# Products over six weight rows in the second MLP matrices, with weight sums made by adding transfers

## The chip, the cores and the metric

The kernel runs on one core of a Trainium2 chip. A core has a matrix engine (TensorE, PE in the profile), a vector engine (VectorE, DVE), an activation engine (ScalarE, ACT), a general engine (GpSimd, POOL) and a queue engine (SyncE, SP); each runs its own list of instructions in order and waits for the others by semaphores. Sixteen DMA engines move data between the chip's memory (HBM) and the core's memory (SBUF); sums of matmuls are held in PSUM, in banks of 128 x 512 float32. The metric is the device time of one execution in microseconds (us), less is better.

## The reference

A two-layer encoder over 256 tokens of width 2048, 16 heads of 128, an MLP of width 8192 in each layer, all in float32:

```python
u = rms_norm(h, a_norm_g[l]); proj = u @ a_w_in[l]           # q, k, v and forget gates
o = forgetting_attention(rms_norm(q), rms_norm(k), v, logf)  # causal, decay bias
h = h + o @ a_w_out[l]
h = h + sq_relu_mlp(h, mlp_norm_g[0], mlp_w1[0], mlp_w2[0])  # (relu(x @ w1) ** 2) @ w2
k_sh, v_sh = split(rms_norm(h, kv_norm_g) @ kv_w)
q = rms_norm(rms_norm(h, b_norm_g[l]) @ b_w_q[l])
o = chunked_relbias_attention(q, k_sh, v_sh, b_rel[l])       # relative position bias
h = h + o @ b_w_out[l]
h = h + sq_relu_mlp(h, mlp_norm_g[1], mlp_w1[1], mlp_w2[1])
```

## The kernel before

**Three passes for float32.** Each matrix operand is cut into a high part and the rest. For a weight tile `issue` (L175) lets ScalarE copy it with rounding into `hi` (L184) and VectorE subtract that into `lo` (L185). A product is then the three passes of `passes` (L402): high by high (L408), high by low activation (L410), low weight by high activation (L412).

**Units.** A weight unit is a tile of 128 x 1024: two weight rows (input tiles of 128) of one output panel of 512 columns. With two blocks of 128 tokens and three passes, `products` (L416) makes twelve matmuls of 512 columns from it. `fetch` (L188) keeps splits up to three units ahead (`AHEAD`), and loads of raw tiles by SP three further. The pool `wsp` has three buffers of `hi` and `lo`, so a split waits until TensorE is through with the unit three before.

**Pairs and formed products.** In the MLP two output panels form a `Pair` (L119). For the first four input tiles (the 2 x 2 blocks of two weight rows by two panels, and two pairs of activation tiles by two token blocks) the pair computes seven products in place of eight, after Strassen and Winograd: "11", T3, T2, T1, "21", T4, "22" (`Form`, L107). T1 to T4 are sums of the weight blocks that VectorE makes (`make`, L747); the sums of the activations come from `sums` (L230). `form_products` (L435) makes six matmuls of one. The remaining input tiles go through plain units, six for each panel (a2 to a7 and b2 to b7).

**The order** is written out: `plan_mlp` (L132) sets the formed products f0 to f6 between the plain units; the last three units of the pair ahead (b5 to b7) lie between f0, f1, f2 and f3. `prepare` (L762) brings the four weight blocks of the next pair (`bring`, L742) and makes T1 and T3 when a given number of plain units is left (`Pair.units`). Two copies of a bank by ScalarE (L853, L856) and two additions by VectorE (L837, L845) join the products in PSUM; the copies stand behind the unit that follows their product. At the end of a matrix panel, VectorE takes the banks (L278, L528), and a list of small tasks, `fill`, is worked off one entry per plain unit (`run_fill`, L197): turning the hidden values by way of DRAM, squaring, splitting, sums.

**Chunks.** The hidden width of 8192 goes in four chunks of 2048; a chunk has two pairs of the first matrix and two of the second, so that a layer's MLP has 16 pairs and the kernel 32.

**The attention** runs as `fill` tasks under the projections. Its biases are loaded by SP (`decay_bias` L709 from a row `cd` written at L695, `rel_bias` L886), into a tile `bias` with two buffers. `begin` (L621) loads and splits the input at the start. POOL has some powers for the head norms (L492) and a few memsets.

Of the kernel before, what the change touches and what calls it, by code (L numbers as in the profile page):

```python
# [31 lines left out]
REL = 384  # L32

# [13 lines left out]
def trunk(ctx: ExitStack, tc: tile.TileContext, xT, xr, gs, hg, bf, wgate, w_in, w_oa, w1a, w2a,  # L47
          w_kv, w_qb, w_ob, w1b, w2b, rel, out):
# [23 lines left out]
    def load_x(i):  # L72
        raw_x[i] = qkv.tile([P, GH, T], F32, name="xin", tag="kv"[i // 2], bufs=2)
        SY.dma_start(raw_x[i], xT[:, i * GH : (i + 1) * GH, :])
# [3 lines left out]
    load_x(0)  # L78

# [4 lines left out]
    ones = const.tile([P, T], F32, name="ones")  # L84
    V.memset(ones, 1.0)
    warm = ps_o.tile([P, 512], F32, name="pt", tag="po")
    for _ in range(11):
        TE.matmul(warm[:, :P], ones[:, :P], ones[:, :P], start=True, stop=True)
# [30 lines left out]
    class Pair:  # L119
# [3 lines left out]
        def __init__(self, src, first, order, third):  # L123
            self.src = [[src[first + q * 8 + u] for u in range(8)] for q in range(2)]
            self.third, self.ps, self.t, self.room, self.units = third, None, {}, None, (9, 8, 7, 6, 5, 2)
            self.head = {"early": "a2 f4 a3 f5 b2 f6 b3 a4 b4 a5 a6 a7", "late": "a2 f4 a3 f5 b2 f6 b3 a4 a5 b4 a6 a7",
                         "": "a2 f4 a3 f5 a4 f6 a5 a6 a7 b2 b3 b4"}[order]

        def items(self, names):
            return [(self, "abf".index(i[0]), int(i[1])) for i in names.split()]  # L130

    def plan_mlp(w1, w2, tail):  # L132
        n, pairs = w1.shape[0] // NCH, []
        for c in range(NCH):
            for src, late in ((w1, ""), (w2, "late")):
                for q in range(2):
                    pairs.append(Pair(src, c * n + 16 * q, (late if pairs else "early") if q == 0 else "", len(pairs) % 2 == 0))
        pairs[0].units, pairs[1].units, pairs[2].units = (15, 13, 11, 8, 10, 8), (9, 8, 7, 6, 3, 2), (9, 8, 7, 6, 1, 2)
        plan, rest = [], [(tail, 0, u) for u in range(KT // UA - 3, KT // UA)]
        for p in pairs:  # L140
            f = p.items("f0 f1 f2 f3")
            plan += [f[0], rest[0], f[1], rest[1], f[2], rest[2], f[3]] + p.items(p.head)
            rest = p.items("b5 b6 b7")
        plan += rest
        units.extend(Form(p, i) if q == 2 else p.src[q][i] for p, q, i in plan)
        return plan
# [6 lines left out]
    plan_a = plan_mlp(w1a, w2a, tail_a)  # L153
# [5 lines left out]
    plan_b = plan_mlp(w1b, w2b, tail_b)  # L159
# [15 lines left out]
    def issue(parts=1):  # L175
        if not raws:
            load(parts)
        raw, cuts = raws.popleft()
        if not cuts:
            raw, cuts = raw.pair.t[raw.name], [slice(0, UN)]  # L180
        hi = wsp.tile([P, UN], F32R, name="hi")
        lo = wsp.tile([P, UN], F32R, name="lo")
        for c in cuts:
            S.activation(hi[:, c], raw[:, c], AF.Copy)  # L184
            V.tensor_tensor(lo[:, c], raw[:, c], hi[:, c].bitcast(F32), op=ALU.subtract)  # L185
        ready.append((hi, lo))

    def fetch(ahead=AHEAD, early=EARLY):  # L188
        while (units or raws) and len(ready) <= ahead:
            issue()  # L190
        while units and sum(1 for r in raws if r[1]) < early:
            load()
        return ready.popleft()
# [36 lines left out]
    def sums(a, fs):  # L230

        w = [wk.tile([P, 512], F32, name="sum", tag="wk") for _ in range(2)]

        def part(i):
            v = w[i // 2][:, i % 2 * 256 : i % 2 * 256 + 256].rearrange("p (g t) -> p g t", g=2)
            return v.rearrange("p g (i c) -> p g i c", i=4) if len(a[0][0].shape) == 4 else v

        V.tensor_tensor(part(0), a[1][0], a[1][1], op=ALU.add)
        V.tensor_tensor(part(1), part(0), a[0][0], op=ALU.subtract)
        V.tensor_tensor(part(2), a[0][0], a[1][0], op=ALU.subtract)  # L240
        V.tensor_tensor(part(3), a[0][1], part(1), op=ALU.subtract)
        hi, lo = ([fs[k][:, i * 512 : (i + 1) * 512] for i in range(2)] for k in range(2))
        for i in range(2):
            S.activation(hi[i], w[i], AF.Copy)
        yield
        for i in range(2):
            V.tensor_tensor(lo[i], w[i], hi[i].bitcast(F32), op=ALU.subtract)
        yield

    def split_turned(t, n, which, into, fs=None):  # L250
        x = acts.tile([P, 2, GH, T], F32R, name="act")
        y = qkv.tile([P, GH, REL], F32, name="bias")[:, :, :T]
# [45 lines left out]
    def turned(name="q"):  # L298
        z = qkv.tile([P, GH * T], F32, name="z")
        return z, qkv.tile([P, GH * T], F32, name=name, tag=name, bufs=2)  # L300
# [52 lines left out]
    class RowStats:  # L353
# [27 lines left out]
        def spread(self):  # L381
            self.R = const.tile([P, T], F32, name="R")
            pr = ps_o.tile([P, 512], F32, name="pt", tag="po")
            rb = wk.tile([P, NB, P], F32, name="rb", tag="wk")
            for b in range(NB):
                V.tensor_scalar(rb[:, b], ones[:, :P], self.r[:, b : b + 1], None, op0=ALU.mult)
# [48 lines left out]
    def form_products(ps, hi, lo, x, fs, i):  # L435
        items = []
        for g in range(2):
            if i in (0, 4, 5):
                xp = [x[2 * g + (i > 0)][:, k, (i == 5) * P : (i == 5) * P + P] for k in range(2)]
            else:  # L440
                c = {3: 0, 2: 1, 1: 2, 6: 3}[i] * 256 + g * P
                xp = [fs[k][:, c : c + P] for k in range(2)]
            items.append((ps[i not in (4, 5)][i in (1, 5)], xp, g, i < 2 and g == 0, i < 2 and g == 1))
# [177 lines left out]
    def begin(u):  # L621
        if u == 0:
            load(2)
            load(2)
# [24 lines left out]
    wgr = const.tile([P, KT * H], F32, name="wgr")  # L649
    ct = {}  # L650

    def gates(x, st):
# [5 lines left out]
        def clear():  # L658
            G.memset(w.bitcast(F32), 0.0)

# [11 lines left out]
        c = const.tile([H, T], F32, name="gc")  # L672

        def logs():
# [14 lines left out]
            V.tensor_tensor_scan(c, ones[:H, :], z, 0.0, op0=ALU.mult, op1=ALU.add)  # L689
# [5 lines left out]
            SY.dma_start(ct["cd"], nct)  # L695
            yield

        def turn_c():
            pc = ps_o.tile([P, 512], F32, name="pt", tag="po")
            ct["cq"] = const.tile([P, NB, H], F32, name="cq")  # L700
            for b in range(NB):
# [5 lines left out]
                [step], [step], [step], [step], [], [turn_c]]  # L707

    def decay_bias(g, box):  # L709
        nb = qkv.tile([P, GH, REL], F32, name="bias")  # L710
        src = ct["cd"][g * GH : (g + 1) * GH, :]
        SY.dma_start(nb, src.unsqueeze(0).to_broadcast([P, GH, REL]))
# [10 lines left out]
    for g in range(NG):  # L723
# [12 lines left out]
        zk, k = turned("k")  # L736
        v = qkv.tile([P, NB, 512], F32, name="v")
# [4 lines left out]
    def bring(p, name):  # L742
        t = qkv.tile([P, UN], F32, name="w" + name, tag="kv"[name[1] == "2"], bufs=2)
        SY.dma_start(t, p.src[int(name[1]) - 1][int(name[0]) - 1])
        p.t[name] = t

    def make(p, name):  # L747
        t = p.t
        if name in ("T1", "T3"):
            if p.room is not None:  # L750
                t[name] = p.room[:, (name == "T3") * UN : (name == "T3") * UN + UN]
            else:
                t[name] = qkv.tile([P, GH * REL], F32, name="w" + name, tag="bias", bufs=2)[:, :UN]
        elif name == "T2":
            t[name] = t["12"]
        else:
            t[name] = t["11"]
        a, b, op = {"T1": ("12", "11", ALU.subtract), "T3": ("22", "12", ALU.subtract),
                    "T2": ("T3", "11", ALU.add), "T4": ("21", "T2", ALU.subtract)}[name]
        V.tensor_tensor(t[name], t[a], t[b], op=op)  # L760

    def prepare(p, d):  # L762
        if d == p.units[0] and p.units[0] > 9:
            p.room = prob.tile([P, 9 * 3 * P], F32, name="wTT", tag="p", bufs=1)
        for name, at in zip(("12", "11", "22", "21", "T1", "T3"), p.units):
# [209 lines left out]
```

## Time and profile before

| | |
|---|---|
| median of 3 runs | 2109.41 us (2108.85 to 2110.25) |
| the profiled execution, its time | 2109.01 us |
| the profiled execution, its span | 2107.2 us |
| TensorE busy in the span | 2099.1 us |
| HBM read, written | 450.01 MB, 39.87 MB |
| mean rate of the DMA engines | 233 GB/s |
| granted clock of TensorE | 1.000 |

The page gives busy times of each engine, then groups of instructions as "line engine operation, out<-in, shapes, count | busy us, mean ns of one | idle before, and what ended it". PE rows overlap by the depth of their pipeline, so that the step from the start of one row to the start of the next is the time to count with. The rows themselves stand in the prediction, where they are used.

### The profile page before, as it was taken

To read this page: it belongs to the slowest core of one execution; us is meant where nothing else is said; L and a number is where in the kernel's file an instruction comes from. 1 tells how busy PE (TensorE), PEld (TensorE's weight loads), DVE (VectorE), ACT (ScalarE), POOL (GpSimd) and SP (SyncE) were. 2 spreads that over 40 slices of the span, in tenths; PEclk is the share of its full clock that TensorE was granted. 3 is DMA by queue.
4 is the path that set the end of the run, shared out by engine and by line. 5 is a ranking of instruction groups with operands and counts; after the bars stand their busy time and mean duration, and the time that the engine had idled before them with its cause. 6 is when DMAs were issued, how large, how long until landed. Compare 5 with 4: busy or idle time off the path is not lost.

```text
span 2107.2 us, 26036 instructions
## 1 busy us (share of the span) xinstructions
PE 2099.1 (100%) x9332; PEld 1741.2 (83%) x9332; DVE 1587.3 (75%) x1812; ACT 1191.4 (57%) x1431; POOL 48.7 (2%) x47
## 2 busy tenths in 40 slices
PE   9999999999999999999999999999999999999999
PEld 8788888888888888888888888888888888888887
DVE  6777676887788777778767677678877877887775
ACT  6545455665466565556575455456654654665653
POOL 1001000000000000000001000000000000000000
PEclk9999999999999999999999999999999999999999
DMA  8787778776676676577678777787766666766774
GB/s 289 236 257 231 234 250 272 241 238 231 216 241 212 211 250 230 188 245 259 194 242 259 238 233 233 227 279 240 257 227 202 232 230 217 236 216 210 244 239 146
DMA packets 182594, 491.63 MB, mean 233 GB/s; under 512 B 36784, under 2 KB 74048, under 8 KB 182464
## 3 DMA queue, kind: packets, MB, share of 16 engines
q1 hardware_dynamic: 182464, 489.96, 71.2%
q8 instruction: 73, 1.20, 0.2%
q14 instruction: 57, 0.47, 0.1%
HBM read 450.01 MB, written 39.87 MB: 232 GB/s over the span
## 4 chain that ended last, share of the span: by engine, by line
PE 99%; DMA 1%; SPq 0%; ACT 0%; DVE 0%; issue 0%; DVEq 0%; ACTq 0%
PE acc L408 26%; PE acc L410 26%; PE acc L412 26%; PE s L408 6%; PE s L412 6%; PE s L410 6%; DMA raw<-in_w_in 1%; PE po L581 1%; PE s L550 1%; PE po L582 0%; PE s L549 0%; PE s L670 0%; DMA turn<-z 0%; SPq L294 0%; ACT hi L184 0%
## 5 line engine op out<-in xcount | busy, mean ns | idle before, releaser
L185 DVE TENSOR_TENSOR lo<-raw,hi 128x1024 fp32r<-128x1024 f32 (+1 forms) x642 | 778.3, 1216 | 296.8 <-ACT hi L184 286.5
L184 ACT ACTIVATE hi<-raw 128x1024 fp32r<-128x1024 f32 (+1 forms) x642 | 677.6, 1057 | 515.2 <-PE acc L410 394.7
L408 PE MATMUL acc<-hi,act 128*128 128x512 f32 x2306 | 632.9, 393 | 2.9 <-ACT hi L184 2.9
L410 PE MATMUL acc<-hi,act 128*128 128x512 f32 x2306 | 623.8, 389 | 0.0
L412 PE MATMUL acc<-lo,act 128*128 128x512 f32 x2306 | 623.5, 389 | 0.0
L410 PEld LDWEIGHTS acc<-hi,act 128*128 128x128 f32 x2306 | 432.8, 188 | 90.4
L412 PEld LDWEIGHTS acc<-lo,act 128*128 128x128 f32 x2306 | 432.8, 188 | 89.9
L408 PEld LDWEIGHTS acc<-hi,act 128*128 128x128 f32 x2306 | 430.8, 188 | 90.9 <-ACT hi L184 3.8
L184 ACT ACTIVATE hi<-w 128x1024 fp32r<-128x1024 f32 x160 | 169.5, 1059 | 153.8 <-PE acc L410 94.4
L185 DVE TENSOR_TENSOR lo<-w,hi 128x1024 fp32r<-128x1024 f32 x160 | 194.8, 1218 | 69.3 <-ACT hi L184 68.3
L408 PE MATMUL s<-hi,act 128*128 128x512 f32 x448 | 121.1, 389 | 0.0
L410 PE MATMUL s<-hi,act 128*128 128x512 f32 x448 | 121.0, 389 | 0.0
L412 PE MATMUL s<-lo,act 128*128 128x512 f32 x448 | 121.0, 389 | 0.0
L184 ACT ACTIVATE hi<-wT 128x1024 fp32r<-128x1024 f32 x60 | 63.6, 1059 | 62.1 <-PE acc L410 41.6
L410 PEld LDWEIGHTS s<-hi,act 128*128 128x128 f32 x448 | 84.1, 188 | 17.5
L412 PEld LDWEIGHTS s<-lo,act 128*128 128x128 f32 x448 | 84.1, 188 | 17.5
L408 PEld LDWEIGHTS s<-hi,act 128*128 128x128 f32 x448 | 84.0, 188 | 17.4
L185 DVE TENSOR_TENSOR lo<-wT,hi 128x1024 fp32r<-128x1024 f32 x60 | 73.2, 1220 | 28.0 <-ACT hi L184 27.8
L760 DVE TENSOR_TENSOR wT<-w,w 128x1024 f32<-128x1024 f32 x60 | 73.1, 1218 | 0.0
L584 ACT ACTIVATE act<-po 128x256 fp32r<-128x256 f32 x32 | 12.3, 385 | 91.1 <-PE po L582 91.1
L492 POOL TENSOR_TENSOR rn<-vv,mhalf 128x4 f32<-128x4 f32 x32 | 43.3, 1366 | 389.9 <-DVE vv L491 389.7
L585 DVE TENSOR_TENSOR act<-po,act 128x256 fp32r<-128x256 f32 x32 | 13.6, 425 | 51.3 <-ACT act L584 51.3
(164 smaller groups left out, 1347.7 us busy)
## 6 DMA issues: line engine op xcount, KB each, us to landing
raw<-in_w_in SPq DMA_DIRECT2D x96, 512.0 KB, 4.5
raw<-in_w1a SPq DMA_DIRECT2D x96, 512.0 KB, 4.3
raw<-in_w2a SPq DMA_DIRECT2D x96, 512.0 KB, 4.4
raw<-in_w1b SPq DMA_DIRECT2D x96, 512.0 KB, 4.3
raw<-in_w2b SPq DMA_DIRECT2D x96, 512.0 KB, 4.3
raw<-in_w_kv SPq DMA_DIRECT2D x64, 512.0 KB, 4.5
turn<-z SPq DMA_DIRECT2D x60, 512.0 KB, 4.2
q<-turn SPq DMA_DIRECT2D x168, 128.0 KB, 3.9
```

The source lines that it names most:

```text
L184: S.activation(hi[:, c], raw[:, c], AF.Copy)
L185: V.tensor_tensor(lo[:, c], raw[:, c], hi[:, c].bitcast(F32), op=ALU.subtract)
L408: TE.matmul(ps[:, cols], xh, cut(hi, j), start=first, stop=False, **kw)
L410: TE.matmul(ps[:, cols], xl, cut(hi, j), start=False, stop=False, **kw)
L412: TE.matmul(ps[:, cols], xh, cut(lo, j), start=False, stop=last, **kw)
L492: G.tensor_tensor(rn, vv, mhalf, op=ALU.pow)
L550: TE.matmul(s[:, P : 3 * P], q[:, a, P:T], k[:, a], start=True, stop=True)
L581: TE.matmul(po[:, :T], v[:, 0, a * P : (a + 1) * P], pT[:, :2], start=True, stop=False)
L584: S.activation(o[i][:, 0], po[:, :T], AF.Copy)
L585: V.tensor_tensor(o[i][:, 1], po[:, :T], o[i][:, 0].bitcast(F32), op=ALU.subtract)
L760: V.tensor_tensor(t[name], t[a], t[b], op=op)
```

## The change

In the pairs of the second matrix, the formed products cover six input tiles in place of four: each block is 128 x 1536 (three weight rows of a panel), `f` is its first two rows (six matmuls) and `h` its third (three). The plain units of such a pair are a3 to a7 and b3 to b7. The weights of the second matrix come in a layout of their own (`_wide`), for each matrix 32 blocks of 1536 columns (`w2f`) and 80 units (`w2s`). The signs of the sums are turned so that every weight sum is an addition; for these pairs T4 is made by a transfer from HBM that adds into the tile of T2 (`put`), and in the second pair of a chunk T1 as well, into the tile of "12". The two bank copies stand directly behind their unit, and a third copy of a bank takes the place of a sign. `hih` and `loh` have one buffer each. The loads of the attention's biases and the row of decays go from SP to POOL, the tile `bias` has one buffer, and some constants lie in it early on. The first input tile is loaded in two halves, with the first weights between. The times of the `fill` tasks are set anew (`uses`, `slots`).

```diff
     class Form:
-        def __init__(self, pair, i):
-            self.pair, self.name = pair, ("11", "T3", "T2", "T1", "21", "T4", "22")[i]
+        def __init__(self, pair, i, half):
+            self.pair, self.name, self.half = pair, ("11", "T3", "T2", "T1", "21", "T4", "22")[i], half
...
+        def plan(self, rest):
+            made = [self.items(f"f{i} h{i}" if self.wide else f"f{i}") for i in range(7)]
+            own = {"early": "a2 F a3 F b2 F b3 a4 b4 a5 a6 a7", "": "a2 F a3 F a4 F a5 a6 a7 b2 b3 b4",
+                   "wide": "a3 F b3 F a4 F b4 a5 a6 a7"}[self.order].split()
+            plan = made[0] + rest[:1] + made[1] + rest[1:2] + made[2] + rest[2:] + made[3]
...
+            for q in range(2):
+                at = 2 * c + q
+                src = [[None] * 3 + [w2s[10 * at + 5 * j + u] for u in range(5)] for j in range(2)]
+                when = (7, 5, 6, 4, 3, 2) if q else (9, 7, 8, 6, 5 if c else 3, 1)
+                pairs.append(Pair({k: w2f[4 * at + i] for i, k in enumerate(names)}, src, "wide", len(pairs) % 2 == 0, when, q == 1))
...
     def issue(parts=1):
...
-            raw, cuts = raw.pair.t[raw.name], [slice(0, UN)]
-        hi = wsp.tile([P, UN], F32R, name="hi")
-        lo = wsp.tile([P, UN], F32R, name="lo")
+            form, half = raw, raw.half
+            raw, cuts = form.pair.t[form.name], [slice(0, 512 if half else UN)]
+            if half:
+                raw = raw[:, UN:]
+        n = cuts[-1].stop
+        hi = wsp.tile([P, n], F32R, name="hi" if n == UN else "hih", bufs=3 if n == UN else 1)
+        lo = wsp.tile([P, n], F32R, name="lo" if n == UN else "loh", bufs=3 if n == UN else 1)
...
+        if form and half == form.pair.wide:
+            if form.name == "T3":
+                make(form.pair, "T2")
+            elif form.name == "T2" and half:
+                put(form.pair, "T4")
...
     def begin(u):
         if u == 0:
             load(2)
+            SY.dma_start(raw_x[0][:, UA:], xT[:, UA:GH, :])
             load(2)
...
-            SY.dma_start(ct["cd"], nct)
+            G.dma_start(ct["cd"], nct)
...
-        SY.dma_start(nb, src.unsqueeze(0).to_broadcast([P, GH, REL]))
+        G.dma_start(nb, src.unsqueeze(0).to_broadcast([P, GH, REL]))
...
     def make(p, name):
...
-        a, b, op = {"T1": ("12", "11", ALU.subtract), "T3": ("22", "12", ALU.subtract),
-                    "T2": ("T3", "11", ALU.add), "T4": ("21", "T2", ALU.subtract)}[name]
-        V.tensor_tensor(t[name], t[a], t[b], op=op)
+        a, b = {"T1": ("12", "11"), "T3": ("22", "12"), "T2": ("T3", "11"), "T4": ("21", "T2")}[name]
+        d, a, b = (t[i][:, : WIDE if p.wide else UN] for i in (name, a, b))
+        V.tensor_tensor(d, a, b, op=ALU.add)
+
+    def put(p, name):
+        at, other = {"T1": ("12", "11"), "T4": ("T2", "21")}[name]
+        p.t[name] = p.t[at]
+        G.dma_start(p.t[name][:, :WIDE], p.big[other], accum_op=ALU.add)
 
     def prepare(p, d):
...
-                (make if name[0] == "T" else bring)(p, name)
+                (bring if name[0] != "T" else put if p.adds and name == "T1" else make)(p, name)
...
             if n == 0:
...
+            elif n == 1:
+                yield from sums([[t3[:, 2 * j + b : 2 * j + b + 1] for j in range(2)] for b in range(NB)], Sh[c][2:], 1)
...
-                form_products(p.ps, hi, lo, p.x, p.fs, u)
-                if u == 0:
-                    make(p, "T2")
-                if u == 2:
-                    V.tensor_tensor(p.ps[0][1], p.ps[1][0], p.t["P7"], op=ALU.add)
+            f, kind, k = plan[i - 1]
+            done = k if i and kind > 1 and kind == 2 + f.wide else None
+            if q > 1:
+                form_products(p.ps, hi, lo, p.x, p.fs, u, q == 3, 1 + p.wide)
+                if u == 1 and q == 2 + p.wide:
+                    p.t["P7"] = wk.tile([P, 512], F32, name="p7", tag="wk")
+                    S.activation(p.t["P7"], p.ps[1][0], AF.Copy)
+                    S.activation(p.ps[1][0], p.ps[1][1], AF.Copy, scale=-1.0)
+                elif u == 2 and q == 2 + p.wide:
+                    V.scalar_tensor_tensor(p.ps[0][1], p.ps[1][0], -1.0, p.t["P7"], op0=ALU.mult, op1=ALU.subtract)
...
-            if i and plan[i - 1][1:] in ((2, 0), (2, 1)):
-                f = plan[i - 1][0]
-                if plan[i - 1][2] == 0:
-                    S.activation(f.ps[0][0], f.ps[1][0], AF.Copy)
-                else:
-                    f.t["P7"] = wk.tile([P, 512], F32, name="p7", tag="wk")
-                    S.activation(f.t["P7"], f.ps[1][1], AF.Copy)
-                    make(f, "T4")
+            if done == 1 and not f.wide:
+                make(f, "T4")
+            elif done == 2:
+                S.activation(f.ps[0][0], f.ps[1][1], AF.Copy)
...
     def rel_bias(g, box):
-        rb = qkv.tile([P, GH, REL], F32, name="bias")
+        rb = room("bias", "rb").rearrange("p (a t) -> p a t", a=GH)
...
-        SY.dma_start(rb[:, :, :T], src)
+        G.dma_start(rb[:, :, :T], src)
```

More of the change, by code (lines that the diff above doesn't have):

```diff
@@ L32 @@
 REL = 384
+WIDE = UN + 512
 def keep_order(tc, engines):
@@ L87, in trunk @@
     for _ in range(11):
-        TE.matmul(warm[:, :P], ones[:, :P], ones[:, :P], start=True, stop=True)
+        TE.matmul(warm[:, :P], ones, ones, start=True, stop=True)
     mhalf = const.tile([P, GH], F32, name="mhalf")
@@ L647, in head_gains @@
         yield
-    wgr = const.tile([P, KT * H], F32, name="wgr")
+    early = room("bias", "early")
+    wgr = early[:, : KT * H]
     ct = {}
```

186 lines of the change are left out of this document (101 added, 85 removed).

## The prediction

> **What bounds the kernel now.** I read the page's shares first, then its chain of work that ended last, then the busy time by stage, then who waited for whom.
>
> ```profile
> PE 2099.1 (100%) x9332; PEld 1741.2 (83%) x9332; DVE 1587.3 (75%) x1812; ACT 1191.4 (57%) x1431; POOL 48.7 (2%) x47
> PE 99%; DMA 1%; SPq 0%; ACT 0%; DVE 0%; issue 0%; DVEq 0%; ACTq 0%
> 420.00:620.00 200.00, 200.00 (x884) 165.64 (x883) 158.76 (x155) 119.20 (x123) 0.00 (x0) 1.00 0.70 230
> 1400.00:1600.00 200.00, 200.00 (x884) 165.66 (x883) 161.46 (x163) 124.23 (x141) 0.00 (x0) 1.00 0.71 238
> PE acc L408 <- ACT hi L184: 2.9, 2, 1.6
> ACT hi L184 <- PE acc L410: 532.4, 483, 3.5
> ```
>
> The columns of the third and fourth line are window, then busy time of PE, weight loads, DVE, ACT, POOL, then granted clock, DMA share, GB/s. In both MLP stages TensorE is busy for all 200 us, at clock 1.00, and it makes 99% of the chain. In the whole span it waited twice for a split weight, 2.9 us in all, while ScalarE waited 483 times for TensorE to give a buffer back. So a matmul taken out is worth its full time, and work added to VectorE (79 to 81% busy there) or ScalarE (60 to 62%) costs nothing until it makes TensorE wait.
>
> The unit price comes from the timeline of TensorE at the first product of a pair:
>
> ```profile
> 375.60 0.62 PE L408 MATMUL s<-hi,act 128*128 128x512 f32 x2
> 376.06 0.61 PE L410 MATMUL s<-hi,act 128*128 128x512 f32 x2
> 376.96 1.07 PE L408 MATMUL acc<-hi,act 128*128 128x512 f32 x4
> 379.68 0.62 PE L408 MATMUL s<-hi,S 128*128 128x512 f32 x2
> ```
>
> A formed product (six matmuls) runs from 375.60 to 376.96, 1.36 us; the plain unit behind it (twelve matmuls) to 379.68, 2.72 us. One matmul of 512 columns is 0.227 us.
>
> **The change, part by part.**
>
> *Matmuls.* A second-matrix pair had 7 formed products of 6 matmuls and 12 units of 12: 186. Now each formed product covers a third weight row (9 matmuls, 2.04 us) and 10 units remain: 63 + 120 = 183. Three fewer in each of 16 pairs is 48, and 48 x 0.227 = **-10.9 us**. TensorE is the bound in these stages, so all of it is gained if no new wait comes.
>
> *Splits and sums on VectorE and ScalarE.* Their durations:
>
> ```profile
> L185 DVE TENSOR_TENSOR lo<-w,hi 128x1024 fp32r<-128x1024 f32 x160 | 194.8, 1218 | 69.3 <-ACT hi L184 68.3
> L184 ACT ACTIVATE hi<-w 128x1024 fp32r<-128x1024 f32 x160 | 169.5, 1059 | 153.8 <-PE acc L410 94.4
> L760 DVE TENSOR_TENSOR wT<-w,w 128x1024 f32<-128x1024 f32 x60 | 73.1, 1218 | 0.0
> L247 DVE TENSOR_TENSOR Sh<-sum,Sh 128x512 fp32r<-128x512 f32 x16 | 10.3, 683 | 0.0
> L244 ACT ACTIVATE Sh<-sum 128x512 fp32r<-128x512 f32 x16 | 10.1, 632 | 17.0 <-DVE sum L239 16.7
> L853 ACT ACTIVATE acc<-s 128x512 f32<-128x512 f32 x16 | 9.3, 582 | 0.0
> ```
>
> A pair loses two splits and gains seven half splits: DVE -2 x 1.22 + 7 x 0.68 = +2.3 us, ACT -2 x 1.06 + 7 x 0.63 = +2.3 us. A weight sum of 1536 columns is 1.5 x 1.218 = 1.83 us (an estimate by length). Four old sums were 4.87 us; the first pair of a chunk now has three on DVE (5.48), the second two (3.65). The sums of the activations for the third row are four short ones and one low half, some 1.9 us a chunk. Over a chunk DVE gets 2 x 2.3 + 0.6 - 1.2 + 1.9 = +5.9 us in about 167 us: 83% instead of 79%. ACT gets one more bank copy (0.58 us) in every pair as well. This is hidden by TensorE as long as each split arrives in time, which I checked by walking one pair.
>
> *One pair walked.* Time 0 is the start of the first product; a plain unit 2.72, a product 1.36, its half 0.68. The halves end at 2.04 (0), 6.80 (1), 11.56 (2), 16.32 (3), 21.08 (4); the plain units between fill the rest. DVE's order in the changed program is: low part of product 1, its half (its only buffer is free at 2.04), the 1.83 us sum T2, low part of the next plain unit, low part of product 2. With DVE free near 2.1 these end near 3.3, 4.0, 5.8, 7.1, 8.3. TensorE needs the plain unit's low part two thirds into it, at 6.80 + 1.81 = 8.6, and product 2's at 10.4: 1.5 and 2.1 us to spare. On ACT the two bank copies behind half 1 run from 6.80 to 8.0; TensorE touches that bank again at 9.52, because a plain unit lies between. Behind them on ACT wait the split of half 2 (done near 8.7, needed at 10.9) and of the next unit (near 9.8, needed at 11.56). Moving the copies forward therefore costs nothing: the split behind them waits for the same product's buffer anyway. If the plain unit did not stand there, it would cost 1.2 us a pair, 37 us over 32 pairs.
>
> *The adding transfers.* T4 = T2 + second weight is now a transfer of 768 KB that POOL issues and that adds into the tile (16 times), T1 of the second pair likewise (8 times). No row shows an adding transfer. The nearest are
>
> ```profile
> w<-in_w2a SPq DMA_DIRECT2D x32, 512.0 KB, 5.3
> bias<-cd SPq DMA_DIRECT2D x4, 768.0 KB, 6.7
> out_h<-h SPq DMA_DIRECT2D x2, 128.0 KB, 1.9
> DMA to landing us min/median/max: 3.5/5.2/8.1
> ```
>
> (issue to landing; the last line is that of the weight tiles). Its deadline from the walk: T2's half is read out near 9.5, so it starts near 9.6; ACT takes 1.06 us for the split that TensorE needs at 23.8, and the low part must follow by 24.7, so it must land by 22.3: **12.7 us**. T1 has 18 us or so. Lower bound of its time: a plain 768 KB, 6.7. Upper: it moves the bytes thrice (read, read, write) against twice, and the slowest tile took 8.1 for two thirds of the bytes; tripling all of that is 24.3. With about 2 us fixed (the 1.9 row) and the median tile, twice the bytes of 1.5 tiles is 2 + 3 x 3.2 = 11.6. I take 9, between that and the plain copy, hidden with 3.7 us to spare; both ends stay for the range. While it is late nothing is lost but what ACT holds behind it. Its load: three puts of 0.79 MB a chunk, counted twice, 4.7 MB in 167 us, is 28 GB/s beside the 230 that took a share of 0.70, so 0.79 at most.
>
> On this transfer the Trainium skill speaks against the change: in "Collectives: The Full Stack", section "The bandwidth ceiling: the fold count and why AG ≠ RS ≠ AR", a reduce in the transfer engines runs at half the rate of a copy, because the addition itself is free but needs two source reads. By that rule the landing is the 11.6 of above and there is no loss; by the plain row it is 6.7 and there is none either; the rule takes away most of what is to spare, and no run here shows it yet.
>
> *Transfers moved from SP to POOL*: nine (the decay row, four decay biases, four relative biases). Behind them on POOL stand only small powers for the head norm. One old stall has to do with SP's order:
>
> ```profile
> SPq L695 <- DVE nct L693: 1.5, 1, 1.5
> SPq L712 <- DMA cd<-nct: 1.4, 1, 1.4
> 73.25 10.75 DMA raw<-in_w_in
> 85.19 1.20 PE L408 MATMUL acc<-hi,act 128*128 128x512 f32 x4 [1.60 <-ACT hi L184]
> ```
>
> SP stood 2.9 us for these two, the weights behind them came late, and TensorE lost 1.6 us at 85. Bounds: all 1.6 gained, or 2 us lost if the bias, now with one buffer, lands later and DVE stands. I take -1.0. All later loads in that queue are nine issues shorter.
>
> *Start.* The first input tile is cut, and the first weights go ahead of its second half:
>
> ```profile
> 1.64 4.83 DMA raw<-in_w_in
> 7.18 0.73 PE L408 MATMUL acc<-hi,act 128*128 128x512 f32 x2 [1.33 <-ACT hi L184]
> ```
>
> 256 KB less stands before 768 KB that took until 6.47. A third of 4.83 would be 1.6; but the second unit needs the other half just as before. Between 0 and -0.9, I take -0.4.
>
> **Sum**: 2109.0 (the profiled execution; its span is 2107.2) - 10.9 - 1.0 - 0.4 = 2096.7. That execution lies 0.4 below the median 2109.4, so 2097 for the median.
>
> **The rivals.**
>
> *Adding transfers land late* (slower). Place: split of product 5, 16 times. Below 12.7 us it costs nothing, beyond it ACT stands in front of that split and TensorE runs dry microsecond for microsecond. The gains of 12.3 us are used up at 12.3/16 = 0.8, so it decides from 13.5 us on. With all of the median tile's time scaled by three, 5.2 x 3 = 15.6, it is 16 x 2.9 = 46 us: 2097 + 46 = 2143. For it: nothing in the trace adds on the way, and the walk's spare is less than the gap between my bounds. Against: POOL's queue is empty in the MLP (0.00 busy above) and the plain row is half the deadline. Chance 0.18.
>
> *VectorE is late behind T2.* The spare of 1.5 us is less than one fill beside it (a low half 1.22, two transposes 1.4, together 2.6). If half of the pairs lose 1.1 us, 8 x 1.1 = 9: 2106. For it: DVE at 81% is the busiest engine behind TensorE, and the 1.83 us sum stands between two splits. Against: ACT and DVE have waited for TensorE far more than the reverse. Chance 0.10.
>
> *POOL's new queue holds up the head norms.* If a bias transfer holds POOL or lands 2 us too late in each of the eight groups, VectorE stands and TensorE loses 16 us: 2113. Five units (13.6 us) lie between issue and the next power, which speaks against it. Chance 0.04.
>
> That the change does not take the work off TensorE is excluded by the count of the instructions.
>
> **How the numbers follow.** The forecast has 0.68, with its own range 2095 to 2103 (both small gains in full, or 6 us of scattered waits). A difference of 0.2% (4.2 us) is what a measurement can tell: faster is below 2105.2, slower above 2113.6. The forecast is faster; the second rival gives 0.04, 0.04, 0.02 (faster, same, slower), the third 0, 0.02, 0.02, the first 0.18 slower. Sums: 0.72, 0.06, 0.22. The range of 8 in 10 goes from 2095 up to 2118, through the second and third rival and the beginning of the first; the far part of the first, up to 16 x 11.6 = 186 us, is left out.
>
> **What will show it.** TensorE busy near 2088, idle still about 8 us. The adding transfers landing in less than 12.7 us, and no wait of "hi" for them that reaches TensorE. The stall at 85 gone or smaller. DVE near 83% in the MLP. It is wrong if TensorE has idle slices in the MLP: next to product 5 it is the transfer, in the plain unit behind T2 it is VectorE, in the attention groups POOL.

## The result, and the profile after

| | before | after |
|---|---|---|
| median of 7 runs each, us | 2109.35 (2108.52 to 2110.25) | 2115.13 (2111.33 to 2119.64) |
| the profiled execution, its time, us | 2109.01 | 2114.63 |
| the profiled execution, its span, us | 2107.2 | 2112.9 |
| matmuls | 9332 | 9284 |

The changed kernel takes 1.0029 times as long (95% interval 1.0017 to 1.0040). It is 5.8 us slower where the forecast was 12 us faster. Its runs also spread over 8 us instead of 2.

Page of the changed kernel: busy time of the engines, then the chain that ended last by engine.

```profile
PE 2096.8 (99%) x9284; PEld 1728.5 (82%) x9284; DVE 1617.3 (77%) x1908; ACT 1230.9 (58%) x1551; POOL 75.2 (4%) x81
...
PE 88%; DVE 5%; DMA 3%; ACT 3%; issue 2%; SPq 0%; DVEq 0%; ACTq 0%
```

The 48 matmuls are gone, but PE's busy time fell by 2.3 us instead of 10.9, and PE's part of the chain fell from 99 to 88%: work of VectorE, ScalarE and the transfers now stands in it. Where this happens is seen in the same two windows of the MLPs as before (PE, weight loads, DVE, ACT, POOL, clock, DMA share, GB/s):

```profile
420.00:620.00 200.00, 198.68 (x872) 163.14 (x872) 161.30 (x167) 122.34 (x136) 2.64 (x3) 1.00 0.75 245
1400.00:1600.00 200.00, 198.69 (x874) 163.28 (x873) 162.77 (x171) 128.42 (x160) 2.59 (x3) 1.00 0.75 246
```

Read the counts rather than the busy time: 872 and 874 matmuls start in 200 us where 884 did, so TensorE got 12 and 10 fewer through, worth 2.7 and 2.3 us at 0.227 each. A busy time of 198.7 hides half of that: a row that waits inside is shown longer (0.73 at 466.52 below, where 0.61 or 0.62 is usual). For the whole span I therefore added up, over all steps of more than 0.25 us from the start of one matmul to the start of the next, what exceeds 0.227 us:

| stretch, us | lost before | lost after |
|---|---|---|
| 0 to 420 | 8.0 | 8.5 |
| 420 to 1080, first MLP | 0.1 | 8.4 |
| 1080 to 1400 | 4.2 | 4.2 |
| 1400 to the end, second MLP | 0.0 | 6.7 |

That is 15.6 us more. The 48 matmuls give back 48 x 0.224 = 10.8 (0.224 is the mean of the undisturbed steps), and that mean is longer by 0.05 ns, 0.5 us in all: 15.6 - 10.8 + 0.5 = 5.3, against the 5.7 by which the spans differ.

Of the 15.1 us lost in the MLPs, 14.0 lie at eight places, one in each chunk: the first pair of its second matrix (2.3, 1.3, 0.5 and 3.3 us near 465, 638, 812 and 967; 2.3, 0.8, 1.2 and 2.4 in the second layer). One later loss, 1.1 us near 1021, is in a second pair. By what TensorE waited for, the 14.0 us are 4.1 for a bank addition of VectorE (L881, behind product 2, in all eight places), 4.0 for the low part of T3 (four places), 3.2 for the low part of the plain unit behind it (six), 1.5 for the second bank copy of ScalarE (L879, seven), and 1.0 for a split half at 967; some 0.2 has no single cause. This is VectorE's list in the first of these places, in its timeline (start, duration, engine, line, operation, tiles; idle time before it in brackets):

```profile
455.59 1.75 DVE L798 TENSOR_TENSOR wT<-w,w 128x1536 f32<-128x1536 f32 x1
457.25 1.22 DVE L212 TENSOR_TENSOR lo<-w,hi 128x1024 fp32r<-128x1024 f32 x1
458.39 1.22 DVE L828 TENSOR_TENSOR act<-q,act 128x1024 fp32r<-128x1024 f32 x1
459.52 0.68 DVE L212 TENSOR_TENSOR loh<-w,hih 128x512 fp32r<-128x512 f32 x1
460.12 1.22 DVE L212 TENSOR_TENSOR lo<-raw,hi 128x1024 fp32r<-128x1024 f32 x1
461.26 0.28 DVE L275 TENSOR_TENSOR sum<-q 128x128 f32<-128x128 f32 x1
...
461.99 0.28 DVE L278 TENSOR_TENSOR sum<-q,sum 128x128 f32<-128x128 f32 x1
462.97 0.69 DVE L284 TENSOR_TENSOR Sh<-sum,Sh 128x512 fp32r<-128x512 f32 x1 [0.70 <-ACT Sh L281]
463.58 1.75 DVE L798 TENSOR_TENSOR w<-w,w 128x1536 f32<-128x1536 f32 x1
465.25 1.22 DVE L212 TENSOR_TENSOR lo<-wT,hi 128x1024 fp32r<-128x1024 f32 x1
466.39 0.68 DVE L212 TENSOR_TENSOR loh<-wT,hih 128x512 fp32r<-128x512 f32 x1
467.10 1.76 DVE L798 TENSOR_TENSOR wT<-wT,w 128x1536 f32<-128x1536 f32 x1
468.78 1.22 DVE L212 TENSOR_TENSOR lo<-raw,hi 128x1024 fp32r<-128x1024 f32 x1
```

The same timeline for ScalarE, and then for TensorE:

```profile
456.54 1.06 ACT L211 ACTIVATE hi<-raw 128x1024 fp32r<-128x1024 f32 x1 [1.14 <-PE acc L450]
462.31 0.63 ACT L281 ACTIVATE Sh<-sum 128x512 fp32r<-128x512 f32 x1 [4.71 <-DVE sum L278]
462.85 1.04 ACT L211 ACTIVATE hi<-wT 128x1024 fp32r<-128x1024 f32 x1
...
468.98 1.06 ACT L211 ACTIVATE hi<-wT 128x1024 fp32r<-128x1024 f32 x1 [2.67 <-DVE wT L798]
```

```profile
459.97 0.62 PE L448 MATMUL s<-hi,act 128*128 128x512 f32 x2
...
465.18 0.61 PE L450 MATMUL s<-hi,Sh 128*128 128x512 f32 x2
466.52 0.73 PE L452 MATMUL s<-lo,Sh 128*128 128x512 f32 x2 [0.73 <-DVE lo L212]
```

The three weight sums T3 (455.59), T1 (463.58) and T2 (467.10), the last split of the hidden values (458.39) and the four sums of them for the third weight row (461.26 on) stand in one train in which VectorE is idle once, for 0.70 us. ScalarE, in order as well, stands 4.71 us at 462.31 for those four sums, with the split of T3 behind it. The low part of T3, wanted by the low pass at 465.6, ends at 466.47, and TensorE stands. Product 0 starts at 459.97, so time 0 of the walk in the prediction is here.

In the kernel before, product 0 of the same pair starts at 459.92. There VectorE makes T3, the split of a plain unit, T1 and then the low part of T3, which ends at 462.62, 2.3 us before TensorE's low pass wants it:

```profile
458.00 1.22 DVE L760 TENSOR_TENSOR wT<-w,w 128x1024 f32<-128x1024 f32 x1
460.27 1.22 DVE L760 TENSOR_TENSOR wT<-w,w 128x1024 f32<-128x1024 f32 x1
461.41 1.21 DVE L185 TENSOR_TENSOR lo<-wT,hi 128x1024 fp32r<-128x1024 f32 x1
...
464.91 0.62 PE L412 MATMUL s<-lo,Sh 128*128 128x512 f32 x2
```

An unbroken train is not the sign in itself: before, VectorE runs here for 22.8 us (448.8 to 471.6) without an idle time above 0.25 us, and the whole first MLP loses 0.1 us. What differs is what stands ahead of the split that is wanted.

Summed over the execution, the waits of the changed kernel that bear on this (who waited, for whom: us, times, longest):

```profile
ACT Sh L281 <- DVE sum L278: 30.3, 8, 4.7
...
DVE nb L758 <- DMA nb<-cd: 7.5, 1, 7.5
...
PE acc L452 <- DVE lo L212: 3.3, 7, 1.7
PE s L452 <- DVE lo L212: 3.0, 4, 0.7
PEld s L448 <- ACT s L879: 2.6, 7, 0.4
...
PE s L448 <- DVE acc L881: 2.2, 8, 0.3
```

Eight waits of up to 4.7 us for L278 are the eight first pairs. The longest of the waits of `acc` for `lo`, 1.7 us, is not in an MLP but at 83.57; PEld is the weight load of a matmul. And these are the adding transfers (the issues with KB each and the median from issue to landing; then the tile `wT`, T4's):

```profile
wT<-in_w2fa POOLq DMA_DIRECT2D x8, 768.0 KB, 7.3
w<-in_w2fb POOLq DMA_DIRECT2D x4, 768.0 KB, 9.3
w<-in_w2fa SPq DMA_DIRECT2D x32, 768.0 KB, 7.7
```

```profile
DMA to landing us min/median/max: 7.1/7.3/8.7
```

The transfers that make T4 land in 7.1 to 8.7 us, those that make T1 (tile `w`) in 9, and a plain load of the same size by SP in 7.7.

### The profile page after: what moved, and what is told of

It is laid out like the page before. It is cut to its first block, busy times and chain, and to the rows that moved or that the text cites. A ratio compares the mean times of both kernels' runs of the same rounds, so it can differ in the third digit from the quotient of the medians.

```text
span 2112.9 us, 26146 instructions
## 1 busy us (share of the span) xinstructions
PE 2096.8 (99%) x9284; PEld 1728.5 (82%) x9284; DVE 1617.3 (77%) x1908; ACT 1230.9 (58%) x1551; POOL 75.2 (4%) x81
## 4 chain that ended last, share of the span: by engine, by line
PE 88%; DVE 5%; DMA 3%; ACT 3%; issue 2%; SPq 0%; DVEq 0%; ACTq 0%
PE acc L448 23%; PE acc L450 23%; PE acc L452 23%; PE s L448 5%; PE s L450 5%; PE s L452 5%; DVE lo L212 2%; ACT hi L211 2%; DMA raw<-in_w1a 1%; DVE wT L798 1%; DMA raw<-in_w1b 1%; PE s L591 1%; PE po L622 1%; DMA turn<-z 0%; ACT act L822 0%
## 5 line engine op out<-in xcount | busy, mean ns | idle before, releaser
L212 DVE TENSOR_TENSOR lo<-raw,hi 128x1024 fp32r<-128x1024 f32 (+1 forms) x610 | 738.2, 1215 | 288.5 <-ACT hi L211 282.8
L211 ACT ACTIVATE hi<-raw 128x1024 fp32r<-128x1024 f32 (+1 forms) x610 | 640.3, 1053 | 351.1 <-PE acc L450 257.7
L448 PE MATMUL acc<-hi,act 128*128 128x512 f32 x2210 | 607.5, 393 | 1.3 <-ACT hi L211 1.3
L452 PE MATMUL acc<-lo,act 128*128 128x512 f32 x2210 | 598.9, 389 | 3.3 <-DVE lo L212 3.3
L450 PE MATMUL acc<-hi,act 128*128 128x512 f32 x2210 | 598.5, 389 | 0.0
L450 PEld LDWEIGHTS acc<-hi,act 128*128 128x128 f32 x2210 | 414.5, 188 | 87.4 <-DVE act L263 0.5
L448 PEld LDWEIGHTS acc<-hi,act 128*128 128x128 f32 x2210 | 412.6, 188 | 85.4 <-ACT hi L211 1.5
L212 DVE TENSOR_TENSOR lo<-w,hi 128x1024 fp32r<-128x1024 f32 x144 | 174.9, 1214 | 50.5 <-ACT hi L211 50.1
L211 ACT ACTIVATE hi<-wT 128x1024 fp32r<-128x1024 f32 x80 | 84.7, 1059 | 95.7 <-DVE wT L798 53.9
L212 DVE TENSOR_TENSOR lo<-wT,hi 128x1024 fp32r<-128x1024 f32 x80 | 97.5, 1219 | 8.6 <-ACT hi L211 6.8
L211 ACT ACTIVATE hih<-w 128x512 fp32r<-128x512 f32 x64 | 40.1, 626 | 46.3 <-PE acc L450 44.1
L625 ACT ACTIVATE act<-po 128x256 fp32r<-128x256 f32 x32 | 12.3, 383 | 84.0 <-PE po L623 84.0
L212 DVE TENSOR_TENSOR loh<-w,hih 128x512 fp32r<-128x512 f32 x64 | 43.9, 686 | 17.7 <-ACT hih L211 17.5
```

Source lines behind the costliest of these rows:

```text
L448: TE.matmul(ps[:, cols], xh, cut(hi, j), start=first, stop=False, **kw)
L450: TE.matmul(ps[:, cols], xl, cut(hi, j), start=False, stop=False, **kw)
L452: TE.matmul(ps[:, cols], xh, cut(lo, j), start=False, stop=last, **kw)
L625: S.activation(o[i][:, 0], po[:, :T], AF.Copy)
```

## The experiments

Three theories stood at the start. **V**: VectorE's train in the first pair of a chunk, with what it makes ScalarE wait for, costs the 15 us. **X**: the transfers (more load on the DMA engines, adding transfers) cost them. **C** (B in an expectation): moving the bank copies forward costs, or saves, something. Later ones have letters in the expectations. Each group of runs had the kernel before on the same chip, at a median of 2107.7 to 2108.0 us, so I compare differences to that; against it the changed kernel is at +5.8. The interval of each difference is 2 to 3 us wide to either side.

### T1 of the first pair by an adding transfer too

```diff
-... Pair(..., when, q == 1)
+... Pair(..., when, True)
```

> T1 of the first second-matrix pair of a chunk is made by an adding transfer too (24 puts become 32; no 1.75 us sum of VectorE between the third-row sums and the split of T3). Theory V (VectorE's unbroken train of three weight sums, third-row sums and splits at the start of the first second-matrix pair makes TensorE wait there): the loss in those pairs falls by up to 1.75 us each in 8 pairs, from 2115 to 2103-2108. Theory X (adding transfers load the DMA engines and make weights land late): eight more of them, 2117-2123.

Measured: 2124.38 us, ratio 1.0073 (1.0057 to 1.0088), +16.7 to before. It takes eight sums of 1.75 us off VectorE and is 11 us slower than the change, which looked like X. The trace says why. First the load between 615 and 630 us (the last two columns are the DMA share and GB/s), then ScalarE's timeline near the stall:

```profile
615.00:620.00 5.00, 5.00 (x24) 4.14 (x23) 3.35 (x5) 3.88 (x6) 0.00 (x0) 1.00 1.02 398
620.00:625.00 5.00, 5.00 (x24) 4.14 (x23) 4.26 (x4) 3.85 (x5) 0.65 (x1) 1.00 1.02 402
625.00:630.00 5.00, 5.00 (x24) 4.14 (x23) 4.96 (x7) 2.01 (x2) 0.20 (x1) 1.00 0.98 227
```

```profile
640.96 1.06 ACT L817 ACTIVATE q<-q 128x1024 f32<-128x1024 f32 x1 [5.25 <-DMA q<-turn]
```

The weight blocks of a first pair are fetched in the stretch in which the hidden values go through DRAM to be turned, and the DMA engines are full there for 15 us (in the changed kernel 1.03, 0.93 and then 0.45, with a mean share of 0.75 over 200 us). With a transfer more, the read of the turned values was issued 10 us after they were written out (4.5 in the changed kernel at the same place), ScalarE stood 5.25 us for them with weight splits behind it, and TensorE stood 2.7 us at 641. So this run doesn't test V: it pays by a transfer in the one place where there is no room for it.

### All sums on VectorE

```diff
-... Pair(..., when, q == 1)
+... Pair(..., when)
-                put(form.pair, "T4")
+                make(form.pair, "T4")
```

> No adding transfer: T4 (16 times) and T1 (8 times) are made by VectorE. V: 24 sums of 1.75 us more on VectorE, the T4 ones right behind T2 in the same train; 10 to 35 us slower than the changed kernel, 2125-2150. X: loads land earlier, 2105-2111.

Measured: 2140.43 us, ratio 1.0158 (1.0145 to 1.0171), +32.8. Without adding transfers it is 27 us slower than with them: the 24 sums that they replace are 24 x 1.76 = 42 us of VectorE, of which 27 show. So the transfers are what makes this change nearly come out even. This alone doesn't show what they cost; runs e5 and e11 below bound it, where all 24 are in place and the MLPs lose 4.2 and 2.9 us in all. So X is not the cause of the 15 us.

### No sums for the third row

```diff
-                yield from sums([...], Sh[c][2:], 1)
+                S.activation(Sh[c][2], t[:, :512], AF.Copy)
+                yield
+                V.tensor_tensor(Sh[c][3], t[:, :512], Sh[c][2].bitcast(F32), op=ALU.subtract)
```

> Leaves out the four short sums of activations for the third weight row (VectorE 1.13 us, four times a layer, and ScalarE's wait for them in front of the weight splits); the hidden values themselves are split in their place. V: 1.1 us and more off the train in 8 pairs, 2106-2111. X: no change, 2113-2117.

Measured: 2105.05 us, ratio 0.9984 (0.9976 to 0.9993), -2.6. Eight times four instructions of 0.28 us, 9 us of VectorE in all, move the time by 8.4, nearly one to one; the loss in the MLPs falls from 15.1 to 4.7 us. This is V, though ScalarE's wait for these sums goes with them.

### The bank copies one unit later

```diff
-                if u == 1 and q == 2 + p.wide:
-                    ...
+            if done == 1:
+                f.t["P7"] = wk.tile([P, 512], F32, name="p7", tag="wk")
+                S.activation(f.t["P7"], f.ps[1][0], AF.Copy)
+                S.activation(f.ps[1][0], f.ps[1][1], AF.Copy, scale=-1.0)
```

> The two bank copies behind product 1 stand one unit later again, in all 32 pairs. If the copies directly behind their unit hold up the splits behind them (theory B): 2105-2110. By the walk of the prediction and V they cost nothing where they are; one unit later they end about when TensorE needs the bank: 2114-2122.

Measured: 2136.47 us, ratio 1.0129 (1.0115 to 1.0144), +28.8, and so 23 us behind the change: the right sign, and a size far above the range expected. TensorE's timeline at the first place:

```profile
474.86 1.22 PE L448 MATMUL s<-hi,Sh 128*128 128x512 f32 x2 [2.35 <-ACT s L893]
475.87 1.05 PE L450 MATMUL s<-hi,Sh 128*128 128x512 f32 x2
476.73 1.05 PE L452 MATMUL s<-lo,Sh 128*128 128x512 f32 x2
477.58 0.63 PE L448 MATMUL s<-hih,Sh 128*128 128x512 f32 x1
```

The copy of the bank (L893) now stands in ScalarE's list behind splits that wait for VectorE, and the product that needs the bank waits 2.35 us for it. The position directly behind the unit is right: over 32 pairs the later one costs 0.7 us a pair.

### The third row's sums on POOL

```diff
-    def sums(a, fs, n=2):
+    def sums(a, fs, n=2, E=None):
+        E = E or V
-        V.tensor_tensor(part(0), ...)
+        E.tensor_tensor(part(0), ...)
...
-                yield from sums([...], Sh[c][2:], 1)
+                yield from sums([...], Sh[c][2:], 1, G)
```

They also start one fill entry earlier, together with the low part of the hidden values.

> The four short sums of activations for the third weight row go from VectorE to POOL, one entry of the task list earlier, so that neither VectorE nor ScalarE stands for them. V: about as good as leaving them out, 6 to 9 us under the changed kernel, 2105-2109. Were it not the sums but the shorter splitting of e3, no change: 2113-2116.

Measured: 2103.09 us, ratio 0.9982 (0.9973 to 0.9991), -4.8. The whole computation is kept, and 10.6 us of the change's time are gone. The group of the last of the four on POOL (count, busy, mean ns, idle):

```profile
L279 POOL TENSOR_TENSOR sum<-q,sum 128x128 f32<-128x128 f32 x8 | 10.3, 1293 | 0.6
```

It takes 1.29 us there against 0.28 on VectorE, and hardly anybody waits for it: all waits of ScalarE for these sums together are 3.9 us (30.3 in the changed kernel). VectorE gets rid of the same 32 instructions as in e3 (1908 down to 1876 in both); the ratios of the two runs, 0.9982 and 0.9984, don't differ beyond their intervals.

### The third panel's tasks later

```diff
-                    uses = (..., (4, 5, 6, 8), (3, 4, 4, 4))[n]
+                    uses = (..., (5, 6, 6, 8), (3, 4, 4, 4))[n]
```

> Only the first two steps of squaring the third hidden panel of a chunk stand later in the task list (entries 5, 6, 6, 8 in place of 4, 5, 6, 8). Theory D (hidden values turned by way of DRAM land late where the loads bunch, and ScalarE stands for them in front of the weight splits): ScalarE's wait for them, 17.8 us in the changed kernel, falls under 8 us and the time by 2 to 5 us, 2109-2112. V alone: no change, 2113-2116.

> Both edits. If V and D hold side by side: 2100-2106, under the kernel before (2108). If they are one and the same loss: as e5 alone.

Alone (e6): 2115.49 us, ratio 1.0040 (1.0028 to 1.0052), +7.6. With the sums on POOL (e7): 2105.24, ratio 0.9983 (0.9974 to 0.9991), -2.7. ScalarE waits less for the turned hidden values (12.3 us in place of 17.8 in the profile of e6), and the time doesn't follow. D (hidden values that come back late from DRAM make ScalarE stand) had expected less than 8 us of these waits, which the edit didn't reach; 5.5 us less of them bought nothing, which speaks against D without excluding it.

### T1 of the first pair on POOL

```diff
-        V.tensor_tensor(d, a, b, op=ALU.add)
+        (G if name == "T1" and p.wide else V).tensor_tensor(d, a, b, op=ALU.add)
```

(on top of e7)

> Both edits, and T1 of the second-matrix pairs that VectorE made (first pair of a chunk, 1.75 us) is made by POOL as an addition of 1536 columns. V: the train shortens by one more sum, 2097-2103, if POOL's reading does not slow VectorE's sums; if it does (VectorE's 1216 ns splits get longer beside it), no better than e7 or worse.

Measured: 2115.49 us, ratio 1.0044 (1.0029 to 1.0059), +7.6, 10 us worse than e7. Two groups of this kernel, then the second of them in the changed kernel, and one of the eight places in e8:

```profile
L801 POOL TENSOR_TENSOR w<-w,w 128x1536 f32<-128x1536 f32 x8 | 35.6, 4456 | 3.5 <-DVE wT L801 3.5
...
L212 DVE TENSOR_TENSOR lo<-w,hi 128x1024 fp32r<-128x1024 f32 x144 | 195.0, 1354 | 60.0 <-ACT hi L211 60.0
```

```profile
L212 DVE TENSOR_TENSOR lo<-w,hi 128x1024 fp32r<-128x1024 f32 x144 | 174.9, 1214 | 50.5 <-ACT hi L211 50.1 <-PE acc L450 0.3
```

```profile
631.21 4.54 DVE L212 TENSOR_TENSOR lo<-w,hi 128x1024 fp32r<-128x1024 f32 x1
...
630.17 4.49 POOL L801 TENSOR_TENSOR w<-w,w 128x1536 f32<-128x1536 f32 x1
```

The addition takes 4.46 us on POOL, and in each of the eight places one instruction of VectorE beside it takes 4.51 to 4.54 us where 1.22 is usual. Six of them are splits of `w`, which explains 195.0 - 174.9 = 20.1 us; two are the low part of the hidden values (L831). In all it is 8 x 3.3 = 26 us. VectorE was to be relieved of 8 x 1.75 = 14.0 us and got 12 more instead.

### T1 of the first pair left out

```diff
     def make(p, name):
         t = p.t
+        if name == "T1" and p.wide:
+            return
```

> Leaves out T1 in the first second-matrix pair of a chunk (the tile of the second weight block is used as it is): 8 sums of 1.75 us fewer on VectorE and no transfer in their place. V: 2104-2109. If 2112 or more, the sum in that place costs nothing by itself, and the losses of e1 and e8, which both take it off VectorE, don't speak of their substitutes alone.

Measured: 2105.90 us, ratio 0.9989 (0.9980 to 0.9998), -2.1. Eight sums of 1.75 us are worth 7.9 us, one microsecond each. With e3 these are two different pieces of work of the same train, and taking either away gives back 8 us. That is what settles V: it isn't a matter of the third row's sums as such. Nor is it ScalarE's wait for them alone, which this run leaves as it was:

```profile
ACT Sh L281 <- DVE sum L278: 30.3, 8, 4.8
```

The waits of TensorE for the low part of T3 (4.0 us in the changed kernel) are gone here; of the 7.2 us that the MLPs still lose, 3.6 are the bank addition of VectorE behind product 2. And this run shows that e1, with the same sums off VectorE, lost by the transfer that took their place: 16.7 + 2.1 = 18.8 us.

### The biases back on SP

```diff
-            G.dma_start(ct["cd"], nct)
+            SY.dma_start(ct["cd"], nct)
```

and `nb` and `rb` likewise; alone (e10) and with the sums on POOL (e11).

> The nine bias transfers (decay row, decay biases, relative biases) go back from POOL to SP; the rest as in the changed kernel. The prediction had the move as a gain of 1.0: then 2114-2117. Theory N (the first decay bias lands later from POOL, VectorE stands 7.5 us for it and TensorE 2 us and more): VectorE's wait for the bias under 2 us, the loss of TensorE between 20 and 100 us not above the 2.5 us of the kernel before, 2110-2113.

Measured: 2115.67 us, ratio 1.0032 (1.0020 to 1.0043), +7.7, no gain. The wait itself did go down, as its row in the list of waits shows (7.5 in the changed kernel):

```profile
DVE nb L758 <- DMA nb<-cd: 2.5, 1, 2.5
```

and in the profiled execution the loss from 20 to 100 us went from 3.1 to 1.2. But that execution, 2111.48 us, is the fastest of the six; one profile doesn't carry a statement on 2 us where runs spread over 6. In the profile of e11, below, where the biases are on SP too, the same loss is 3.9.

> The edits of e5 and e10 together. V and N side by side: 2098-2102, with less spread than e5 (2101.7 to 2108.3), as no run then has the long stall near 82 us. N wrong: as e5, 2102-2105.

Measured: 2102.47 us, ratio 0.9973 (0.9962 to 0.9984), -5.5, from 2100.99 to 2104.62. This is the best version, better than both kernels. Its windows:

```profile
420.00:620.00 200.00, 199.65 (x878) 164.13 (x877) 161.61 (x164) 123.70 (x137) 5.66 (x7) 1.00 0.74 244
1400.00:1600.00 200.00, 199.62 (x877) 164.09 (x877) 163.88 (x170) 129.69 (x157) 5.82 (x7) 1.00 0.74 242
```

VectorE is as busy in these windows as in the changed kernel (161.6 against 161.3, 163.9 against 162.8), while TensorE gets 878 and 877 matmuls through: its share of busy time says nothing about the loss, the order of its work does. Nor does the length of its trains: at the first of the eight places its list has 20.1 us without a gap here (451.4 on), and TensorE loses 0.9. The loss in the two MLPs is 1.4 + 1.5 us. Between e11 and e5 the intervals overlap, so that the part of the biases in it stays open.

## Why the prediction was wrong

**The walk's start is the step that failed.** "With DVE free near 2.1" was assumed, not read from the list of what stands there: in the first pair of a chunk VectorE still has a plain unit's split, the third row's sums, their low half and T1 to do, and is free at 463.58 + 1.75 - 459.97 = 5.4. Everything behind it is then 2.9 to 3.2 us late, more than the spare of 1.5 and 2.4 us that the walk leaves:

| low part of | forecast | needed | measured |
|---|---|---|---|
| product 1 | 3.3 | 5.7 | 6.5 |
| (T2 made) | 5.8 | | 8.9 |
| the plain unit behind it | 7.1 | 8.6 | 10.0 |

(measured from the timeline above, 459.97 taken off; needed from the prediction's own walk, the first as 4.76 + 0.91.) In the second pair T1 and the third row's sums aren't there, and one pair in eight lost something. The walk was right for that pair and was used for both: with product 0 at 503.85, VectorE is free at 2.4 there and the three parts end at 3.6, 6.0 and 7.2. The walk also ended too early: the bank addition behind product 2, which costs most (4.1 of the 14.0 us), was not in it.

**"83% instead of 79%"** was too high rather than too low (161.3 and 162.8 of 200 us, 81% in both windows shown; over the execution VectorE got 30.0 us more, where 8 x 5.9 = 47 were forecast) and proved nothing: what counts is what stands ahead of a split when it is wanted. Runs e3 and e12 show that this train is on the path, where a microsecond off VectorE gives 0.6 to 0.9 back (7.9 of 14.0, 8.4 of 9, the second with ScalarE's wait gone as well).

**ScalarE's part** was walked for the bank copies alone. That its third-row split stands 4.7 us ahead of the weight splits was not seen. e3 and e5 take this wait and a part of VectorE's train away together. e12 leaves the wait and takes 7.9 of the 15 us away by VectorE's length alone; how much of the rest goes by the wait stays open.

**The second rival was the right mechanism** (VectorE late), at a chance of 0.10, though for another reason: not a fill beside T2, but the work ahead of it. The time lies in the stated range because that reached up to 2118 for this rival and the third; the forecast itself was a gain. The rival's size was too small: 8 x 1.1 = 9 against 14.0 in eight places, 1.75 each. With this term in place of it the prediction's sum comes out: 2109.0 - 10.8 + 15.0 in the MLPs + 0.5 in the first 420 us + 0.5 in the mean step = 2114.2, against 2114.6 measured; as its parts are measured ones, this says only that nothing large is left over. The mark given for it, TensorE idle in the plain unit behind T2, is there (a step of 0.68 at 469.4, 3.2 us in six places); the loss one product ahead of it (4.0) and that behind product 2 (4.1) are larger.

**Matmuls**: right. 48 fewer, 10.8 us, and e11 makes half of that visible.

**The adding transfers** were right and the first rival falls: 7.3 us for T4 where 9 was taken, below 12.7 in the slowest case (8.7). In the Trainium skill, "Collectives: The Full Stack", section "The bandwidth ceiling: the fold count and why AG ≠ RS ≠ AR", a reduce in the transfer engines has half the rate of a copy. Here the landing doesn't show that rule: the adding transfer for T4 landed as fast as a plain one of 768 KB (7.3 against 7.3 to 7.7). The time of the DMA engines does show it. In e10 POOL's queue (q0) has nothing but the adding transfers, and their packets took 1.9 times as long per MB as those of the plain queue (packets, MB, share of the engines):

```profile
q1 hardware_dynamic: 178000, 489.96, 68.1%
q0 software_dynamic: 3456, 18.88, 5.0%
```

Counting their load twice, as the prediction did, was right. The load was forecast at 0.79 at most and measured at 0.75 on the mean; that it reaches 1.03 and 0.93 in two windows of 5 us (0.88 and 0.89 before) was not looked for, and e1, with a third such window, pays for it.

**Bank copies**: that moving them forward costs nothing is nearly right. The two copies run from 10.0 to 11.2 in the first pair shown (469.94 to 471.14) instead of 6.8 to 8.0, behind T2's split, which stands for VectorE; TensorE's weight loads wait for the second one, 2.6 us in seven places, which costs 1.5 of the 14.0 us. That their place matters was missing: one unit later costs 23 us (e4), by ScalarE waits for VectorE that the walk left out.

**Biases and start**: -1.0 was forecast for the biases, and nothing measurable came. SP no longer stands for the row `cd`, but the decay bias came 7.5 us late for VectorE, and the old stall of 1.98 us (the step between matmul starts at 83) is one of 2.09 at 81. That VectorE stands for the bias was the bad end of this term, and it cost no more than the old stall. At the start the first weight matmul went from 7.18 to 6.69, 0.5 where 0.4 was forecast, and the first 420 us lost 0.5 us more all the same.

**The third rival** (POOL's queue ahead of the head norms) left no trace: from 1080 to 1400 us, where the second attention runs, the loss is 4.2 as before.

**Open**: why the waits saved in e10 don't show in its time; why the changed kernel spreads over 8 us; why e7, which differs from e5 by the third panel's tasks alone, ran at 2.1 us less gain, within both intervals.

## What to carry to other kernels

A share of busy time is no cover: walk the in-order list of the second engine through the densest stretch of a period, starting from the work that really stands ahead of it and going on until the list is level again, and do it once for each variant of the period. Work that is added must be placed by which list has a gap just there; 9 us of short sums moved to an idle engine were worth 10.6 us here, as much as the 48 matmuls. For transfers the same holds: look at the load over 5 us too, as e1 shows, and not only at the mean over 200.

## What the runs showed of the hardware

After some stalls TensorE runs at about half its rate. In e4, 2.35 us idle at 474.86 were followed by steps of 0.86 us for two matmuls (475.87 to 476.73 to 477.58 above), 0.43 for one where 0.227 is usual. In the profile of e5 a stall of 3.6 us at 82 was followed by about a dozen steps of 0.427, some 6 us, and in e1 one of 2.7 at 641 by eight; a stall of 2.09 at 81 in the changed kernel had one step of 0.34 behind it and then the usual rate, and in e8 one of 1.9 at 464 was followed by eight slow steps again; another of 2.7 in e1, at 1695, was followed by none. So the length of the one stall doesn't decide. The Trainium skill, "TensorE: Matmul & The Clock Gate", section "What's actually happening", tells of a gate that halves the clock after an idle window of about 3.4 us and opens it after a busy one; the step of 0.427 and the length of some 3.4 us in e1 and e8 agree, while stalls of 1.9 to 2.7 us were enough here. Such a stall can cost 1.7 times its length: in e1, 4.2 us from 641 to 648 for one of 2.5 us beyond the usual step.

POOL and VectorE kept each other waiting on instructions with two inputs in SBUF. In e8 the split that VectorE began at 631.21, during POOL's addition, ended 1.1 us after that addition (635.75 against 634.66), nearly its whole usual time; POOL's addition had begun under an instruction of VectorE that ended at 631.28, so that some 3.4 of its 4.49 us are its own (an estimate from these rows), against 1.75 on VectorE. The Trainium skill, "SBUF — State Buffer", section "SBUF: two separate sides", has the two share a port pair that one holds for its whole instruction, VectorE when it has two inputs in SBUF; the trace agrees. The four short sums of 128 columns (0.45 to 1.4 us each on POOL in e5 and e11) did no harm that the time shows.
